# A two-layer streaming encoder step: a tie on the first load of cached keys, the queue of half the key stores, and the instants of the prompt's attention blocks

## Chip, cores and metric

The kernel runs on one core of a Trainium2 chip. The metric is the device time of one launch in microseconds (us), lower is better. The core has a matmul engine (PE, with its weight loads listed as PEld), a vector engine (DVE), a scalar engine (ACT) and GpSimd (POOL); SyncE (SP) only issues DMAs. Each of SP, ACT and POOL issues its DMAs in order; an instruction that waits at the head of an engine's queue holds up all behind it on that engine.

## What is computed

Two layers over 512 prompt rows and 8 x 16 sample rows of width 1024, in float32. Layer 0 is a gated MLP with a spatial mix, layer 1 is attention with a forget bias over 16 heads of 128. The part that matters here is layer 1:

```python
q, k, v, z, logf = fox_project(h, w_in, b_f)          # h: normalised rows; k and v are outputs too
s = q @ k.T * scale + c_q - c_k                        # c: running sum of logf; causal
o = softmax(s) @ v                                     # prompt: 512 keys; sample: 256 cached keys and 16 new ones
x = x + rms_norm((o * silu(z)) @ w_out)
x = x + sigmoid(x @ w_gate) * (p @ w_proj)
```

The outputs are both sets of rows, the new keys and values and log-forget values of both groups, and a state of layer 0.

## The kernel before, in words

Float32 products are split in two parts (`split`, lines 285 to 292: ACT makes the high part, DVE the low part), and a product is three matmuls (`mm3`, 269). The projections of layer 1 use a scheme of seven products on half-sized blocks (`seven_products`, 556): per projection 7 x 4 steps of three matmuls, each step counted as 0.441 planner units. POOL forms the weight sums for it (`left_operands`, 203, line 210), and the weights of layer 1 come by DMAs on POOL's queue (`fetch`, 197), apart from the first four units, which go on SP.

Layer 1 runs in rounds of two heads, p = 0 to 7 (line 1183). A round's steps are the z projection of pair p and the v, k and q projections of pair p + 1; together 4 x 28 x 0.441 = 49.4 units. Beside them, `interleave` (356) traces pieces of attention, each at an instant written by hand in units. Pieces whose instant lies past the last step are traced at the end of the round. The order in which the program is traced is a priority: a scheduler then orders each engine's instructions by its own estimate of when they are ready, and may put a ready one ahead. Where that is not wanted, `queued("sp")` (127) adds an edge: what is traced inside it stays behind `behind["sp"]`, the SP DMA that was traced last (`dma`, 120, sets it), in issue order.

Pieces of a round: two heads of the prompt (`prompt_times`, 1123), each with a setup, four blocks of 128 queries (`scores`, 992), their transposes (`turn`, 7.5 units later) and products with v (`values`, 12.5 later). The first block of the even head is at t0 and a block follows every `step` units; the odd head starts four steps later. `scores` is one matmul group, then on DVE a mask addition (994), an addition with minimum (1004, 1007), the reciprocal (1014) and the scaling (1015), with the exponential on ACT (1010). Then two groups of four sequences of the sample (`sample_times`, 1132). Cached keys come in 32-column pieces, four DMAs per half pair (`load_k`, 1038, on SP, each 128 KB), and DVE turns them (`turn_k`, 1050, line 1054). New keys are stored by `store_k` (919): a DVE transpose (920), then eight DMAs per head, on POOL's queue. The finished head's rows go to DRAM by `store_y` (1136, POOL).

Ahead of the rounds, `tail(0, ...)` ends layer 0: it stores the five residual blocks to `x_sc` on SP (758) as they are done. `project_v0` (885) is the first projection of layer 1; its `weights(2)` (243) takes the first v weights, and with them fetches the next units, the last of them on SP being the k weights of pair 0. Beside it run the forget logits, the sums of h (`right_operands`, 426, line 432: it overwrites the residual's buffers) and the first `load_k(0, 0, 0)`, at 1.0 units, into buffers that the residual blocks used.

Of the kernel before, what the change touches and what calls it, by code (L numbers as in the profile page):

```python
# [57 lines left out]
def hybrid_trunk(tc, x_prompt, x_sample, ck, cv, clf, p_prompt, p_sample, norm_pre, norm_post,  # L58
                 g_win, ln_g, ln_b, w_s, b_s, g_wout, f_win, b_f, f_wout, w_proj, w_gate, consts,
                 y_p, y_s, st_v, fk_p, fv_p, fl_p, fk_s, fv_s, fl_s):  # L60
    nc = tc.nc
# [28 lines left out]
    def r1(o, n, p=P):  # L90
        return R1[:p, o:o + n]
# [11 lines left out]
    def bank(lst=(0, 1, 2, 3, 4, 5, 6, 7)):  # L103
        return PB[ring(("bank", lst), lst)]
# [15 lines left out]
    def dma(out, in_, queue=None):  # L120
        if queue is not None:
            queue.dma_start(out=out, in_=in_)  # L122
        else:
            behind["sp"] = nc.sync.dma_start(out=out, in_=in_)

    @contextmanager
    def queued(*engines):

        with ExitStack() as stack:
            for e in engines:  # L130
                stack.enter_context(tc.issue_after(behind[e].ins))
            yield
# [110 lines left out]
    def weights(n):  # L243

        i0 = state["used"]
        state["used"] += n
        prefetch(i0 + 2 * NW, i0)
        res = []
        for i in range(i0, i0 + n):
            u, j = items[i]  # L250
            k, o, m = units[u][1], place[i][0] * 1024, len(place[i]) * 512
            if u in joined:
                res.append(W[:, o:o + 2 * m].rearrange("p (k n) -> p k n", k=k))
                continue
            if j in (1, 2):
                views = [W[:, o + z:o + z + m].rearrange("p (a k n) -> p k a n", a=2, k=k) for z in (0, m)]
            else:
                views = [W[:, o + z:o + z + m].rearrange("p (k n) -> p k n", k=k) for z in (0, m)]
            res.append(tuple(views))
        return res  # L260
# [69 lines left out]
    def h_at(k, a, b):  # L330
        return h_hi[:, k, a:b], h_lo[:, k, a:b]
# [24 lines left out]
    def interleave(steps, pieces):  # L356


        now, todo = 0.0, sorted(pieces, key=lambda x: x[0])
        for took in steps:  # L360
            now += took
            while todo and todo[0][0] <= now:
                todo.pop(0)[1]()
        for _, piece in todo:
            piece()
# [492 lines left out]
    def v_of(p):  # L858
        return r1(o_v + (p % 2) * 1280, 1280).rearrange("p (t n) -> p t n", t=NT)

    def both(o, i):
        return r1(o + i * TOK, TOK)
# [19 lines left out]
    def store_v(p, t):  # L882
        dma(fv_rows(p, t), v_of(p)[:, t].rearrange("p (h d) -> p h d", h=2))

    def project_v0():
        v = v_of(0)
        ws = weights(2)
        for t in range(NT):
            b = bank(PRJ)
            for k in range(8):  # L890
                w = ws[k // 4][:, k % 4]
                hi, lo = h_at(k, t * P, (t + 1) * P)
                nc.tensor.matmul(b, hi, w, start=k == 0, stop=False)
                nc.tensor.matmul(b[:, :256], lo, w[:, :256], start=False, stop=k == 7)
                if k % 2:
                    yield 0.69
            nc.scalar.activation(out=v[:, t], in_=b[:, 256:], func=AF.Copy)
            nc.vector.tensor_tensor(out=v[:, t], in0=v[:, t], in1=b[:, :256], op=ALU.add)
            store_v(0, t)
# [17 lines left out]
        yield from seven_products(lambda i, j: both(o_vk, i)[:, HALF[j]], lambda i, j, c: None)  # L917

    def store_k(h, tr):
        nc.vector.transpose(out=tr, in_=both(o_k, h % 2))  # L920
        trv = tr.rearrange("p (c d) -> p c d", d=32)
        for qd in range(4):
            dma(fk_p[0, 0, :, h, qd * 32:(qd + 1) * 32].rearrange("(c j) d -> j c d", j=32), trv[qd * 32:(qd + 1) * 32, :16], nc.gpsimd)
            dma(fk_s[0, :, :, h, qd * 32:(qd + 1) * 32].rearrange("(c b) q d -> (b q) c d", c=4), trv[qd * 32:(qd + 1) * 32, 16:], nc.gpsimd)

    def project_k0():
        ws = weights(2)
        n = TOK - SA
        for h in range(2):
            a, b = yield from channel_steps(ws, h, PRJ)  # L930
            kt = both(o_k, h)
            nc.scalar.activation(out=kt[:, :SA], in_=a[:, :SA], func=AF.Copy)
            nc.scalar.activation(out=kt[:, SA:], in_=b[:, n:], func=AF.Copy)
            behind["dve"] = nc.vector.tensor_tensor(out=kt[:, SA:], in0=kt[:, SA:], in1=b[:, :n], op=ALU.add)
            store_k(h, both(o_vk, h))
# [32 lines left out]
    def w0_of(h):  # L968
        return tri if h % 2 else SF[:, 2048:2560] if h < 14 else r1(o_raw, 512)

    def load_w0(h, queue=None):
        dma(w0_of(h), c_sc[h].partition_broadcast(P), queue)
# [65 lines left out]
    def load_k(p, bg, hh):  # L1038
        for qd in range(4):
            d = slice(qd * 32, (qd + 1) * 32)  # L1040
            dma(kraw[d].rearrange("p b (c d) -> p (b c) d", d=32),
                ck[0, 4 * bg:4 * bg + 4, :, 2 * p + hh, d].rearrange("b (c j) d -> j (b c) d", j=32))

    def load_v(p, bg):
        for z in range(2):
            b = 4 * bg + 2 * z
            dma(vv[:, 2 * z:2 * z + 2].rearrange("p b t n -> p (b t) n"),
                cv[0, b:b + 2, :, 2 * p:2 * p + 2, :].rearrange("b (t k) h d -> k (b t) (h d)", k=P))

    def turn_k(p, bg, hh):  # L1050

        with queued("dve"):
            for bl in range(4):
                nc.vector.transpose(out=kt[:, hh, bl, :PAST], in_=kraw[:, bl])  # L1054

    def new_k(p, bg):
        for hh in range(2):
            nc.gpsimd.tensor_copy(out=kt[:, hh, :, PAST:], in_=kn_of(2 * p + hh)[:, 64 * bg:64 * bg + 64].rearrange("p (b k) -> p b k", b=4))
# [64 lines left out]
    def prompt_times(h, t0, step):  # L1123

        setup, scores, turn, values = prompt_pieces(h)
        res = [(t0 - step + 0.1, setup)]
        for i in range(4):
            for after, f in ((0, scores), (7.5, turn), (12.5, values)):
                res.append((t0 + step * i + after, lambda f=f, i=i: f(i)))
        return res  # L1130

    def sample_times(p, bg, t0):
        scores, turn, values, gate = sample_pieces(p, bg)
        return [(t0, scores), (t0 + 7.5, turn), (t0 + 12.5, values), (t0 + 17.5, gate)]

    def store_y(h):
        dma(y_sc[h], y_of(h), nc.gpsimd)
# [12 lines left out]

    def attention_pieces(p, step, s1):

        s0, t0 = 5, 3.2
        pieces = sample_times(p, 0, s0) + sample_times(p, 1, s1)
        ka, kb = 5, 17.6
        pieces += [(s0 + ka, lambda: turn_k(p, 1, 0)), (s0 + ka + 0.1, lambda: load_k(p, 1, 1)), (s0 + kb, lambda: turn_k(p, 1, 1)),
                   (s0 + kb + 0.1, lambda: new_k(p, 1)), (s0 + 13.5, lambda: load_v(p, 1))]
        for hh in range(2):
            pieces += prompt_times(2 * p + hh, t0 + 4 * step * hh, step)
        if p < 7:  # L1160
            pieces += [(s1 + 18, lambda: store_y(2 * p)), (s0 + kb + 0.2, lambda: load_k(p + 1, 0, 0)), (s1 + 13.5, lambda: load_v(p + 1, 0))]
        if p == 6:
            pieces += [(48, lambda: load_w0(14)), (48, lambda: load_w0(15))]
        return pieces

    def next_keys(p, t, t_new):

        return [(t, lambda: turn_k(p, 0, 0)), (t + 0.1, lambda: load_k(p, 0, 1)), (t + 12, lambda: turn_k(p, 0, 1)),
                (t + 12.1, lambda: load_k(p, 1, 0)), (t_new, lambda: new_k(p, 0))]
# [3 lines left out]
    def sums_of_h():  # L1173
        sums.append(right_operands((o_P, o_v + 1280, o_V, o_qp, o_z)))

    interleave(project_v0(), [(0.0, forget_logits), (2.0, log_forget), (2.1, sums_of_h), (9.0, forget_sums),
                              (9.1, lambda: load_w0(0, nc.gpsimd)), (1.0, lambda: load_k(0, 0, 0))])
    interleave(project_k0(), [(11.0, lambda: turn_k(0, 0, 0)), (11.1, lambda: load_k(0, 0, 1)), (0.0, lambda: load_w0(1, nc.gpsimd)), (0.1, lambda: load_mask(0, nc.gpsimd)), (6.0, lambda: load_v(0, 0))])
    split(*quarter(0, 1), sums[0])
    nc.gpsimd.memset(r1(o_qp, 512), 0.0)  # L1180
    interleave(project_q(0), [(8.0, lambda: turn_k(0, 0, 1)),
                              (8.1, lambda: load_k(0, 1, 0)), (12.2, lambda: new_k(0, 0))])
    for p in range(7):
        pieces = attention_pieces(p, 4.7, 26.0) + next_keys(p + 1, 34.0, 46.2)
        pieces += [(26.0, lambda p=p: turn_v(p + 1, 0)), (27.0, lambda p=p: turn_v(p + 1, 1))]
        interleave(project(project_z(p), project_v(p + 1), project_k(p + 1), project_q(p + 1)), pieces)
        store_y(2 * p + 1)
# [4 lines left out]
    pieces = attention_pieces(7, 5.2, 24.7)  # L1192
# [39 lines left out]
```

## Time and profile before

| | us |
|---|---|
| median of 3 runs | 1310.72 (1309.7 to 1311.1) |
| profiled execution, its own time | 1311.3 |
| its span, first to last instruction | 1309.5 |
| PE busy | 1282.0 (98%) |
| DVE busy | 964.2 (74%) |
| ACT busy | 587.7 (45%) |
| POOL busy | 426.7 (33%) |

In lists of groups, a row gives line, engine, operation, out<-in, shapes and count, then busy us, mean ns of one, and the idle time just before them with what ended it. In the timeline a row gives start and duration in us, then the instruction, a count when several follow each other, and in brackets the idle time before it and what ended it. In stretches a row gives the bounds, the length, each engine's busy time with its count, the clock granted to PE as a share of full speed, the busy share of the 16 DMA engines, and GB/s. SPq is SP's queue. Buffers: `R` is the large work buffer, `W` the split weights, `RAW` the weights as they arrive, `pb` the banks of PSUM.

### The profile page before, as it was taken

Reading aid. Unit: us, or ns where it says so; the run is one execution under the profiler, and the core shown is the slowest. Engines: PE = TensorE matmul, PEld = TensorE weight load, DVE = VectorE, ACT = ScalarE, POOL = GpSimd, SP = SyncE. Lnnn points to the kernel's source line nnn. Section 1 sums busy time; section 2 is a strip of 40 time slices with the busy share of each in tenths; the row PEclk is TensorE's granted clock in tenths of the full one; section 3 lists DMA queues with packets and bytes.
Section 4 is the critical chain, followed back from the end, with each engine's and each line's share of the span. In section 5 each row is a group of like instructions: output and inputs, shape, how many; then the busy total and the mean of one; then the engine's idle time right before and its main releaser. Section 6 shows DMA issues by size and latency. Waiting matters only on the chain. (4 is left out here: it accounts for less than half of the span.)

```text
span 1309.5 us, 21108 instructions
## 1 busy us (share of the span) xinstructions
PE 1282.0 (98%) x7873; PEld 1144.3 (87%) x7873; DVE 964.2 (74%) x1808; ACT 587.7 (45%) x1062; POOL 426.7 (33%) x455
## 2 busy tenths in 40 slices
PE   9999999999999999898999999999999999999998
PEld 6888999999988888787898989898988989888887
DVE  7744999999844364696979798988879797744643
ACT  5334555444535343354444354544444454535431
POOL 1012454543000000345554646465545552000100
PEclk9999999999999999998999999999999999999999
DMA  6432334232324213546787667676787667742111
GB/s 228 132 108 67 119 114 127 79 110 75 128 83 160 81 49 103 141 99 139 155 170 154 171 157 174 137 187 126 167 151 167 145 167 209 262 141 81 65 57 57
DMA packets 236353, 171.53 MB, mean 131 GB/s; under 512 B 147801, under 2 KB 198537, under 8 KB 236250
## 3 DMA queue, kind: packets, MB, share of 16 engines
q1 hardware_dynamic: 218162, 122.54, 33.1%
q0 software_dynamic: 14176, 42.14, 15.4%
q10 hardware_dynamic: 3912, 5.50, 1.3%
q8 instruction: 62, 1.02, 0.3%
q14 instruction: 41, 0.34, 0.1%
HBM read 148.55 MB, written 21.59 MB: 130 GB/s over the span
## 5 line engine op out<-in xcount | busy, mean ns | idle before, releaser
L271 PE MATMUL pb<-A,W 128*128 128x320 f32 (+1 forms) x752 | 241.0, 321 | 10.3 <-DVE R L578 4.6
L273 PE MATMUL pb<-A,W 128*128 128x320 f32 (+1 forms) x752 | 235.3, 313 | 0.6 <-DVE W L292 0.6
L272 PE MATMUL pb<-A,W 128*128 128x320 f32 (+1 forms) x752 | 235.7, 313 | 0.0
L289 DVE TENSOR_TENSOR W<-RAW,W 128x1024 fp32r<-128x1024 f32 (+1 forms) x126 | 146.7, 1165 | 85.6 <-ACT W L288 83.4
L271 PE MATMUL pb<-W,A 128*128 128x512 f32 x520 | 205.1, 395 | 0.7 <-ACT A L288 0.7
L272 PE MATMUL pb<-W,A 128*128 128x512 f32 x520 | 204.1, 393 | 0.0
L273 PE MATMUL pb<-W,A 128*128 128x512 f32 x520 | 202.8, 393 | 0.0
L288 ACT ACTIVATE W<-RAW 128x1024 fp32r<-128x1024 f32 (+1 forms) x126 | 120.0, 952 | 107.3 <-PE pb L273 47.0
L271 PEld LDWEIGHTS pb<-A,W 128*128 128x128 f32 x752 | 142.7, 190 | 14.2 <-DVE R L578 5.4
L272 PEld LDWEIGHTS pb<-A,W 128*128 128x128 f32 x752 | 142.8, 190 | 1.3 <-issue 1.2
L273 PEld LDWEIGHTS pb<-A,W 128*128 128x128 f32 x752 | 142.3, 189 | 0.8 <-DVE W L292 0.8
L301 POOL TENSOR_TENSOR SML<-SML 128x1 f32<-128x1 f32 x25 | 18.5, 742 | 372.7 <-DVE SML L299 368.0
L271 PE MATMUL pb<-tbf,W 128*128 128x320 f32 x360 | 117.0, 325 | 0.7 <-ACT W L288 0.3
L273 PEld LDWEIGHTS pb<-W,A 128*128 128x128 f32 x520 | 98.0, 189 | 21.0 <-issue 0.8
L271 PEld LDWEIGHTS pb<-W,A 128*128 128x128 f32 x520 | 98.1, 189 | 20.4 <-ACT A L288 1.1
L272 PEld LDWEIGHTS pb<-W,A 128*128 128x128 f32 x520 | 98.2, 189 | 19.4
L273 PE MATMUL pb<-tbf,W 128*128 128x320 f32 x360 | 112.4, 312 | 1.4 <-DVE W L289 1.2
L272 PE MATMUL pb<-tbf,W 128*128 128x320 f32 x360 | 113.0, 314 | 0.0
L562 DVE TENSOR_TENSOR R<-R,pb 128x320 f32<-128x320 f32 x184 | 85.7, 476 | 23.1 <-PE pb L273 22.0
L210 POOL TENSOR_TENSOR sff<-RAW 128x512 f32<-128x512 f32 x46 | 62.1, 1350 | 88.4 <-DVE W L289 41.1
L122 POOL DMA_DIRECT2D out<-R x128 | 78.2, 618 | 17.2 <-DMA RAW<-in_fox_w_in 10.2
L1010 ACT ACTIVATE R<-R,SML 128x128 f32<-128x128 f32 (+1 forms) x64 | 35.8, 560 | 94.8 <-DVE SML L1007 94.4
(271 smaller groups left out, 2887.9 us busy)
## 6 DMA issues: line engine op xcount, KB each, us to landing
RAW<-in_fox_w_in POOLq DMA_DIRECT2D x46, 512.0 KB, 6.4
RAW<-in_gmlp_w_in SPq DMA_DIRECT2D x40, 512.0 KB
R<-in_cache_fox_k SPq DMA_DIRECT2D x128, 128.0 KB
R<-in_cache_fox_v SPq DMA_DIRECT2D x32, 512.0 KB
RAW<-in_gmlp_w_out SPq DMA_DIRECT2D x16, 512.0 KB
RAW<-in_ple_w_gate SPq DMA_DIRECT2D x16, 512.0 KB
RAW<-in_fox_w_out SPq DMA_DIRECT2D x16, 512.0 KB
R<-in_fox_w_in POOLq DMA_DIRECT2D x14, 512.0 KB, 7.8
```

The source lines that it names most:

```text
L122: queue.dma_start(out=out, in_=in_)
L210: nc.gpsimd.tensor_tensor(out=o, in0=a, in1=b, op=op)
L271: nc.tensor.matmul(out, lh, rh, start=start, stop=False)
L272: nc.tensor.matmul(out, lh, rl, start=False, stop=False)
L273: nc.tensor.matmul(out, ll, rh, start=False, stop=stop)
L288: nc.scalar.activation(out=hi, in_=src, func=AF.Copy)
L289: nc.vector.tensor_tensor(out=lo, in0=src, in1=f(hi), op=ALU.subtract)
L301: nc.gpsimd.tensor_tensor(out=q, in0=t, in1=mhalf, op=ALU.pow)
L562: behind["dve"] = nc.vector.tensor_tensor(out=into(i, j), in0=a, in1=b, op=ALU.add)
L1010: nc.scalar.activation(out=pr[:, :n], in_=pr[:, :n], func=AF.Exp, scale=-1.0, bias=m, accum_out=sm)
```

## The change

Three edits. The first `load_k` of layer 1 is traced inside `queued("sp")`. `store_k` gives its eight DMAs no queue, which means SP, for the even heads from 2 on; heads 0 and 1 and the odd ones stay on POOL. The prompt's first block of a round moves from 3.2 to 4 units in all eight rounds, and the step from 4.7 to 4.8 in rounds 0 to 6 (round 7 keeps 5.2).

```diff
     def store_k(h, tr):
+        queue = nc.gpsimd if h < 2 or h % 2 else None
         nc.vector.transpose(out=tr, in_=both(o_k, h % 2))
         trv = tr.rearrange("p (c d) -> p c d", d=32)
         for qd in range(4):
-            dma(fk_p[...], trv[qd * 32:(qd + 1) * 32, :16], nc.gpsimd)
-            dma(fk_s[...], trv[qd * 32:(qd + 1) * 32, 16:], nc.gpsimd)
+            dma(fk_p[...], trv[qd * 32:(qd + 1) * 32, :16], queue)
+            dma(fk_s[...], trv[qd * 32:(qd + 1) * 32, 16:], queue)
...
     def attention_pieces(p, step, s1):
 
-        s0, t0 = 5, 3.2
+        s0, t0 = 5, 4
...
+    def first_k():
+        with queued("sp"):
+            load_k(0, 0, 0)
+
     interleave(project_v0(), [(0.0, forget_logits), (2.0, log_forget), (2.1, sums_of_h), (9.0, forget_sums),
-                              (9.1, lambda: load_w0(0, nc.gpsimd)), (1.0, lambda: load_k(0, 0, 0))])
+                              (9.1, lambda: load_w0(0, nc.gpsimd)), (1.0, first_k)])
...
     for p in range(7):
-        pieces = attention_pieces(p, 4.7, 26.0) + next_keys(p + 1, 34.0, 46.2)
+        pieces = attention_pieces(p, 4.8, 26.0) + next_keys(p + 1, 34.0, 46.2)
```

More of the change, by code (lines that the diff above doesn't have):

```diff
@@ L922, in store_k @@
         for qd in range(4):
-            dma(fk_p[0, 0, :, h, qd * 32:(qd + 1) * 32].rearrange("(c j) d -> j c d", j=32), trv[qd * 32:(qd + 1) * 32, :16], nc.gpsimd)
-            dma(fk_s[0, :, :, h, qd * 32:(qd + 1) * 32].rearrange("(c b) q d -> (b q) c d", c=4), trv[qd * 32:(qd + 1) * 32, 16:], nc.gpsimd)
+            dma(fk_p[0, 0, :, h, qd * 32:(qd + 1) * 32].rearrange("(c j) d -> j c d", j=32), trv[qd * 32:(qd + 1) * 32, :16], queue)
+            dma(fk_s[0, :, :, h, qd * 32:(qd + 1) * 32].rearrange("(c b) q d -> (b q) c d", c=4), trv[qd * 32:(qd + 1) * 32, 16:], queue)
     def project_k0():
```

## The prediction

> **What bounds the kernel now.** I read the page first, then busy time by stretches, then the waits of the matmul engine (PE).
>
> ```profile
> span 1309.5 us, 21108 instructions
> PE 1282.0 (98%) x7873; PEld 1144.3 (87%) x7873; DVE 964.2 (74%) x1808; ACT 587.7 (45%) x1062; POOL 426.7 (33%) x455
> ```
>
> PE is busy for 98% of the span, so the idle time that any reordering can win back is 1309.5 - 1282.0 = 27.5 us, plus the time that PE ran at a lower clock. The profiled execution took 1311.3 us, 1.8 above its span; the median of the three runs shown is 1310.72, so 0.6 below this execution. The attention loop has eight rounds of two heads, p = 0 to 7. The busy time of rounds 0 to 6, cut where each round's first matmul of the z projection starts:
>
> ```profile
> core 0: us, PE busy (x) PEld busy (x) DVE busy (x) ACT busy (x) POOL busy (x), PEclk, DMA share, GB/s
> 589.05:667.00 77.95, 72.21 (x506) 66.07 (x506) 61.52 (x141) 35.12 (x67) 44.31 (x51) 0.96 0.74 155
> 667.00:738.36 71.36, 69.96 (x508) 63.66 (x507) 61.20 (x139) 32.16 (x65) 42.64 (x49) 1.00 0.77 162
> 738.36:808.66 70.30, 68.27 (x508) 63.58 (x507) 60.97 (x137) 32.41 (x64) 39.33 (x46) 1.00 0.63 155
> 808.66:878.57 69.91, 68.80 (x508) 63.73 (x507) 57.83 (x141) 33.12 (x66) 37.86 (x45) 1.00 0.75 169
> 878.57:950.30 71.73, 69.95 (x508) 63.67 (x507) 62.30 (x139) 32.16 (x65) 41.18 (x48) 1.00 0.70 150
> 950.30:1022.27 71.97, 68.79 (x509) 63.52 (x507) 60.94 (x139) 32.67 (x65) 39.70 (x47) 1.00 0.77 158
> 1022.27:1092.17 69.90, 68.78 (x509) 63.73 (x507) 57.72 (x138) 33.33 (x66) 35.84 (x42) 1.00 0.67 164
> ```
>
> Rounds 1 to 6 lie between 69.90 and 71.97, and round 0 needs 8.05 more than the best. Everything after the start of the loop is therefore worth little per round; the dear spots are ahead of round 0 and in it. PE's two longest waits, from the timeline (start, duration, then the idle time before it and what ended it), and the stretches of 10 us around them:
>
> ```profile
> 551.69 0.44 PE L271 MATMUL pb<-A,W 128*128 128x384 f32 x1 [3.64 <-DVE R L898]
> ```
> ```profile
> 607.88 0.63 PE L271 MATMUL pb<-A,W 128*128 128x320 f32 x1 [3.28 <-DVE R L578]
> ```
> ```profile
> 550.00:560.00 10.00, 8.31 (x44) 7.83 (x45) 9.97 (x12) 0.53 (x1) 0.00 (x0) 0.83 0.15 52
> 600.00:610.00 10.00, 6.72 (x40) 6.46 (x39) 4.28 (x18) 3.71 (x8) 4.96 (x5) 0.84 0.92 199
> 610.00:620.00 10.00, 9.64 (x54) 9.07 (x53) 10.00 (x24) 6.96 (x16) 3.38 (x3) 0.82 0.53 96
> ```
>
> Each time PE waits for the vector engine (DVE). The granted clock (the column after POOL) falls behind both long stalls: 0.17 x 10 = 1.7 us of clock behind the first, 0.16 x 10 + 0.18 x 10 = 3.4 behind the second. Together the two spots cost 3.64 + 1.7 + 3.28 + 3.4 = 12.0 us.
>
> **Part 1, the tie of the first K load: 0 us.** The queue of SyncE (SP) and DVE's wait at this place:
>
> ```profile
> 501.67 8.14 SPq L124 DMA_DIRECT2D RAW<-in_fox_w_in  x4
> ...
> 535.38 5.42 SPq L124 DMA_DIRECT2D R<-in_cache_fox_k  x4
> 540.90 3.08 SPq L124 DMA_DIRECT2D x_sc<-R  x1
> ```
> ```profile
> 549.53 1.78 DVE L432 TENSOR_TENSOR R<-A 128x1280 f32<-128x1280 f32 x1 [7.16 <-issue]
> ```
>
> The four parts of the K load go out ahead of the last residual store (`x_sc`), which is issued 5.5 us later and whose buffer one of the additions of line 432 overwrites. DVE stands still for 7.16 us until 549.53 (the view names no releaser; I read it as that store's landing), and PE's stall of 3.64 follows. A tie behind that store would go at this. But `queued("sp")` ties to `behind["sp"]`, the SP DMA traced last. When `first_k` runs, one step of `project_v0` has been traced, whose `weights(2)` has fetched the units of the first K projection on SP, after `tail` had traced all `x_sc` stores. So the tie is to the last of the four `in_fox_w_in` fetches (501.67 and the 8.14 us after it), and the K load at 535.38 stands behind that already. A tie that the order meets changes no order: SP still issues four K parts, then the store, and no queue is passed. Bounds: 0, and -12.0 if the tie reached the store and both spots vanished. I take 0. What would be late next, had the first stall gone, is the second, which has another cause:
>
> ```profile
> 605.05 0.63 ACT L288 ACTIVATE W<-RAW 128x512 fp32r<-128x512 f32 x1 [8.71 <-DMA RAW<-in_fox_w_in]
> ```
>
> This waits for a weight fetch on POOL's queue, in a stretch where the DMA engines are 0.92 busy; heads 0 and 1 keep their stores on POOL, so nothing here moves.
>
> **Part 2, K stores of heads 2, 4 ... 14 from POOL to SP: -1.0 us.** Eight DMAs per head:
>
> ```profile
> L122 POOL DMA_DIRECT2D out<-R x128 | 78.2, 618 | 17.2 <-DMA RAW<-in_fox_w_in 10.2
> ```
> ```profile
> 933.63 5.00 POOL L122 DMA_DIRECT2D out<-R  x8
> ...
> 947.72 0.76 POOL L122 DMA_DIRECT2D RAW<-in_fox_w_in  x1
> ...
> 951.06 0.57 POOL L122 DMA_DIRECT2D y_sc<-R  x1 [0.38 <-DVE R L1030]
> ```
> ```profile
> 949.72 15.54 DMA R<-in_cache_fox_k
> ```
> ```profile
> L124 SPq DMA_DIRECT2D R<-in_cache_fox_k x98: 312/560/6493, 665.6 to 1091.4; - x98
> ...
>   DVE R L1054: 2.6, 3
> ```
>
> Removed from POOL: 7 x 8 x 0.618 = 34.6 us, 4.9 per round, none of it on PE's path, since POOL is busy for 33%. Added to SP: 56 issues at 0.56 (the median of its K loads), 31 us, also off the path. Queued behind them on SP are the loads of V and K, which are due at 39.5 and 46.1 planner units where the stores come at 35.3, four and eleven units later (a unit is 70 us / 49.4 = 1.42 us), against 8 x 0.56 = 4.5 us of issue; the stores wait only for DVE's transposes of line 920. The gain can come from order: the fetch at 947.72 stands behind sixteen stores, and the K load issued just after it took 15.54 us to land. Five us earlier it would largely be through before the K load starts. DVE waited for K loads 2.6 us in 3 places in rounds 1 to 6: the gain is at most that, plus what the better landing saves downstream. On the other side, the stores now share SP's queue with K loads. If each of the seven heads' stores held the next K load back by those 4.5 us, that would be 31 us of landing; the turns that need it come 12 units (17 us) later, so most is covered, and I bound the loss by the same 2.6. I take -1.0, nearer to the gain, since the fetch and K load of 947 to 965 are in the trace and a wait behind a store is not.
>
> The rule that speaks against this part is in the Trainium skill, DMA: Bandwidth & Descriptors, "Issuing engines are not separate DMA queues": whichever engine starts them, DMAs run on the same 16 DMA engines, and another issuer saves only issue time. By it the sum would be 1.0 higher; no run here separates the two yet.
>
> **Part 3, blocks of the prompt at 4.0 and every 4.8 units: -2.4, and -0.3 in round 0.** The middle of round 3, and four of DVE's groups in that round (count, busy us, mean ns):
>
> ```profile
> 822.66:846.66 24.00, 22.89 (x165) 21.27 (x165) 23.96 (x51) 13.35 (x25) 13.52 (x11) 1.00 0.65 146
> ```
> ```profile
> L1015 DVE TENSOR_SCALAR R<-R,SML 128x128 f32<-128x128 f32 (+3 forms) x8 | 3.9, 485 | 0.1
> L1004 DVE CUSTOM_DVE_ANT_0 R<-pb,sff 128x128 f32<-128x128 f32 (+2 forms) x3 | 1.3, 419 | 1.5 <-PE pb L273 1.5
> L994 DVE TENSOR_TENSOR CST<-CST 128x128 f32<-128x128 f32 x2 | 1.1, 569 | 0.0
> L1014 DVE RECIPROCAL SML<-SML 128x1 f32<-128x1 f32 x8 | 1.2, 152 | 1.4 <-ACT R L1010 1.4
> ```
>
> PE's idle time in this stretch, 24.00 - 22.89 = 1.11 us, is all that the round has (69.91 - 68.80), and DVE is full in it: 23.96 of 24. In the other 45.91 us DVE works 57.83 - 23.96 = 33.87 and has room. Work that is pushed from the full stretch into the last one shortens DVE's backlog. The instants of the blocks in it go from 7.9, 12.6, 17.3, 22.0, 26.7 to 8.8, 13.6, 18.4, 23.2, 28.0 units, 1.1 later on average, 1.56 us. A block's DVE work is the mask addition (0.569), the addition with minimum (0.419, twice except in a head's first block), the reciprocal (0.152) and the scaling (0.485): 8 x 1.625 + 6 x 0.419 = 15.5 us per round, 0.22 us per us. The backlog falls by 1.56 x 0.22 = 0.34 us per round, 2.4 in seven. Bounds: no more than the idle time of rounds 1 to 6 (425.17 - 414.55 busy = 10.6), and as much the other way. In round 0 DVE does a block's work right ahead of the sum that PE waits for at 607.88:
>
> ```profile
> 606.33 0.28 DVE L994 TENSOR_TENSOR R<-sff,CST 128x128 f32<-128x128 f32 x1
> 606.53 0.28 DVE L1004 CUSTOM_DVE_ANT_0 R<-pb,sff 128x128 f32<-128x128 f32 x1
> ```
>
> If the later block falls behind the sum, that saves at most 0.56; I take half.
>
> The last `values` goes from 48.6 to 50.1 units, past the 28 x 4 x 0.441 = 49.4 of the steps, so it is traced at the end of the round. The fourth block also loads a head's mask row on ACT's queue, 1.1 to 1.5 units later now, for a block 35 units on; that is covered. The four matmuls of `values` are only moved; the DVE product behind them and `store_y` of the odd head come about 1.5 units later, 2.1 us. The first z sum that overwrites the stored buffer comes after four products, 7.06 units or 10 us into the round.
>
> ```profile
> y_sc<-R POOLq DMA_DIRECT2D x14, 320.0 KB, 4.5
> ```
>
> In round 5 the store goes out 0.76 us into the round; with 2.1 more and the median landing of 4.5 it is through at 7.4. That hides it by 2.6 us; a landing twice as long would cost DVE 1.9 us in a round, in a stretch where it has room. In round 7 (steps of 5.2) the last `values` goes from 52.1 to 52.9, 7 units ahead of the interleave's end at 59.95; nothing there waits.
>
> Sum: 0 - 1.0 - 2.4 - 0.3 = -3.7, so 1311.3 - 3.7 = 1307.6 for an execution like the profiled one and 1307.0 as a median.
>
> **The rivals.**
> (a) The tie does reach the residual store. For it: DVE's 7.16 us end about where the late store would land. Against: what was traced last on SP. It would give at least the first stall with its clock, 5.3, so 1307.0 - 5.3 = 1301.7, and up to 1295.0. Chance 0.07.
> (b) Round 0's stall shrinks by 0.3 to 0.6 and the clock stays up behind it: -3.4, 1303.6. Against: at 3.28 it already cost 3.4. Chance 0.06. The Trainium skill, TensorE: Matmul & The Clock Gate, part 1, has the clock halve after an idle window of about 3.4 us; the trace has it fall behind a stall of 3.28, so the measurement decides.
> (c) Nothing measurable: POOL's time was free, the backlog is rebuilt in another order, and the two dear spots stay. 1308.1 to 1313.3. Chance 0.22.
> (d) Slower: the first block of the odd head goes from 22.0 to 23.2 units and is now behind the last turn of cached K at 22.6, so that it stands on DVE behind a wait for that K load. The point that decides is a landing of over (22.6 - 10.1) x 1.42 = 17.7 us after the load's due time, and 15.54 has been seen. The price is that each of rounds 1 to 6 takes the pattern of the worst: 6 x 71.97 - 425.17 = +6.7, 1317.4, or half of it, 1314. Against: three waits for K in six rounds. Chance 0.23.
>
> **How the numbers follow.** My forecast has 0.42. About 0.2% (2.6 us) is what a measurement can tell from no change. Faster: 0.42 + 0.07 + 0.06 = 0.55; same 0.22; slower 0.23. The forecast's own range is 1303 to 1308.1; the range given, 1301 to 1315, adds (b), (c) and the nearer half of (a) and (d).
>
> **What would show it.** Right: SP still issues four K parts ahead of the last `x_sc` store near 535, PE still stalls about 3.6 us near 551 and about 3 near 607, clock rows under 0.85 at both; POOL has 72 stores of K and SP 56 more; rounds 1 to 6 near 70.4. Wrong: the store ahead of the K load and no stall at 551 (then (a)); rounds over 72 with DVE waiting for K loads ahead of line 1004 (then (d)); a round 0 under 74 without any change of SP's order.

## The result and the profile after

The changed kernel takes 1298.88 us (median of 6 runs, 1297.73 to 1300.96) against 1310.63 for the kernel before (6 runs beside them): a ratio of 0.9913, 95% interval [0.9901, 0.9926]. That is 11.7 us less, where 3.7 had been forecast, and outside the range. The profiled execution's page begins with the span and the busy time of the engines:

```profile
span 1297.4 us, 21121 instructions
PE 1276.6 (98%) x7873; PEld 1144.2 (88%) x7873; DVE 975.8 (75%) x1808; ACT 588.8 (45%) x1062; POOL 398.8 (31%) x399
```

PE's busy time fell by 5.4 us, though it does the same 7873 matmuls; DVE's rose by 11.6. The rounds, cut at the same matmul as before, are the first seven rows, and the eighth is everything behind them:

```profile
589.14:665.97 76.83, 70.58 (x507) 64.85 (x506) 60.41 (x143) 35.23 (x67) 39.86 (x43) 0.98 0.76 157
665.97:734.82 68.85, 68.23 (x510) 63.71 (x508) 62.13 (x139) 32.84 (x66) 40.35 (x42) 1.00 0.83 174
734.82:802.99 68.17, 68.17 (x510) 63.80 (x508) 62.47 (x139) 32.61 (x66) 34.67 (x39) 1.00 0.69 164
802.99:871.15 68.16, 68.16 (x509) 63.78 (x508) 62.68 (x138) 32.60 (x66) 34.08 (x39) 1.00 0.73 162
871.15:939.76 68.61, 68.37 (x510) 63.73 (x508) 61.93 (x141) 32.61 (x66) 32.93 (x36) 1.00 0.77 152
939.76:1011.87 72.11, 70.06 (x509) 64.67 (x508) 63.47 (x139) 32.73 (x66) 40.31 (x42) 0.98 0.81 171
1011.87:1080.04 68.17, 68.17 (x510) 63.79 (x508) 59.44 (x135) 32.92 (x66) 31.09 (x34) 1.00 0.64 156
1080.04:1297.40 217.36, 213.01 (x1101) 177.99 (x1099) 116.80 (x220) 90.12 (x159) 5.11 (x8) 1.00 0.36 121
```

The loop starts where it did (589.14 against 589.05) and what follows the seven rounds is as long (217.36 against 1309.5 - 1092.17 = 217.33). The whole gain lies in the rounds: 1080.04 - 589.14 = 490.90 against 503.12. In three of them PE has no idle time left, and they are shorter than PE's *busy* time was before (68.17 against 68.27 to 69.96). Only round 5 stayed at 72.

What the tie should have touched is where it was. SP's queue, then PE's two long stalls, then the stretches of 10 us around them:

```profile
535.23 5.44 SPq L124 DMA_DIRECT2D R<-in_cache_fox_k  x4
540.77 3.45 SPq L124 DMA_DIRECT2D x_sc<-R  x1
```
```profile
551.79 0.69 PE L271 MATMUL pb<-A,W 128*128 128x384 f32 x1 [3.96 <-DVE R L898]
...
607.73 0.41 PE L271 MATMUL pb<-A,W 128*128 128x320 f32 x1 [3.19 <-DVE R L578]
```
```profile
550.00:560.00 10.00, 8.21 (x44) 7.71 (x45) 9.96 (x12) 0.43 (x1) 0.06 (x1) 0.83 0.15 52
600.00:610.00 10.00, 6.73 (x42) 6.20 (x42) 4.44 (x18) 3.88 (x9) 4.89 (x5) 0.97 0.92 198
610.00:620.00 10.00, 9.11 (x52) 8.19 (x51) 10.00 (x24) 6.80 (x14) 3.53 (x4) 0.86 0.55 98
```

Four K parts still go ahead of the last residual store, and both stalls are there. Behind the second the granted clock lost 0.3 + 1.4 = 1.7 us where it had lost 3.4. Round 0 is 1.1 us shorter (76.83 against 77.95).

Where the rounds differ is seen in the stretch from 3.5 to 14 us into round 3, first before, then after (the fifth column is DVE):

```profile
812.16:822.66 10.50, 10.50 (x83) 9.66 (x82) 5.96 (x21) 1.86 (x6) 5.80 (x7) 1.00 0.68 159
```
```profile
806.49:816.99 10.50, 10.50 (x82) 9.66 (x81) 9.76 (x25) 3.95 (x8) 4.25 (x6) 1.00 0.47 115
```

DVE had a hole here, 5.96 us of work in 10.5, right ahead of the 24 us in which it is full (23.96 of 24). Now the hole is filled, and ACT does twice as much in it. The work that moved in is the split of the next weights (ACT line 288, DVE 289), which needs POOL's sums of line 210. POOL's timeline around the same place, before and after:

```profile
813.00 0.76 POOL L122 DMA_DIRECT2D R<-in_fox_w_in  x1 [2.33 <-issue]
815.02 0.24 POOL L1058 COPY R<-R 128x64 f32<-128x64 f32 x1 [1.26 <-PE pb L1078]
...
815.68 1.29 POOL L210 TENSOR_TENSOR sff<-RAW 128x512 f32<-128x512 f32 x1
817.05 1.30 POOL L210 TENSOR_TENSOR sff<-sff,RAW 128x512 f32<-128x512 f32 x1
818.43 1.30 POOL L210 TENSOR_TENSOR sff<-RAW,sff 128x512 f32<-128x512 f32 x1
```
```profile
801.87 1.27 POOL L210 TENSOR_TENSOR sff<-RAW 128x512 f32<-128x512 f32 x1 [0.95 <-DVE W L289]
...
804.85 1.41 POOL L210 TENSOR_TENSOR sff<-sff,RAW 128x512 f32<-128x512 f32 x1
...
807.00 1.30 POOL L210 TENSOR_TENSOR sff<-RAW,sff 128x512 f32<-128x512 f32 x1
```

Round 3 starts at 808.66 before and at 802.99 after. The second to fourth sums of this set came 7.0 to 9.8 us into the round and now come from 1.1 us ahead of it to 4.0 us into it.

### The profile page after: what moved, and what is told of

It is laid out like the page before. It is cut to its first block, busy times and chain, and to the rows that moved or that the text cites. A ratio compares the mean times of both kernels' runs of the same rounds, so it can differ in the third digit from the quotient of the medians.

```text
span 1297.4 us, 21121 instructions
## 1 busy us (share of the span) xinstructions
PE 1276.6 (98%) x7873; PEld 1144.2 (88%) x7873; DVE 975.8 (75%) x1808; ACT 588.8 (45%) x1062; POOL 398.8 (31%) x399
## 4 chain that ended last, share of the span: by engine, by line
PE 44%; DVE 4%; DMA 2%; issue 1%; POOL 1%; ACT 0%; DVEq 0%; SPq 0%; ACTq 0%
PE pb L271 12%; PE pb L272 12%; PE pb L273 12%; PE pb L1029 2%; PE pb L1022 1%; PE pb L1106 1%; DMA RAW<-in_fox_w_in 1%; DVE W L289 1%; PE pb L1079 1%; DVE R L1055 1%; DMA R<-in_fox_w_in 1%; PE pb L906 1%; DVE R L959 0%; POOL sff L210 0%; DMA R<-in_cache_fox_k 0%
## 5 line engine op out<-in xcount | busy, mean ns | idle before, releaser
L289 DVE TENSOR_TENSOR W<-RAW,W 128x1024 fp32r<-128x1024 f32 (+1 forms) x126 | 160.9, 1278 | 80.4 <-ACT W L288 77.7
L289 DVE TENSOR_TENSOR A<-R,A 128x640 fp32r<-128x640 f32 (+1 forms) x42 | 34.4, 854 | 58.2 <-ACT A L288 58.2
L271 PEld LDWEIGHTS pb<-tbf,W 128*128 128x128 f32 x360 | 68.1, 189 | 9.3 <-issue 6.2
```

Source lines behind the costliest of these rows:

```text
L271: nc.tensor.matmul(out, lh, rh, start=start, stop=False)
L289: nc.vector.tensor_tensor(out=lo, in0=src, in1=f(hi), op=ALU.subtract)
```

## The experiments

**The three parts alone.** Each is the kernel before with one part of the diff. The first has the tie:

```diff
+    def first_k():
+        with queued("sp"):
+            load_k(0, 0, 0)
```

> Part 1 alone on the kernel before. Theory (the tie is to a weight fetch that SP issues earlier anyway): ratio 1.000 within 0.1%, PE stalls of about 3.6 us near 551 and 3.2 near 607 stay, SP issues the four K parts ahead of the last x_sc store. Rival (the tie reaches the store): 5 to 12 us faster, and the stall near 551 is gone.

1310.44 us against 1310.46, ratio 1.0001 [0.9992, 1.0011]. The tie does nothing.

The second has the stores:

```diff
+        queue = nc.gpsimd if h < 2 or h % 2 else None
```

> Part 2 alone on the kernel before (even heads' K stores on SP, instants as before). POOL theory: the eight store issues are what held POOL's weight sums (line 210) back; without them the sums stand about 8 us earlier in a round, the splits fill the idle stretch of DVE 4 to 14 us into the round, and most of the 11.7 us comes: 1299 to 1303. Instants theory (part 3 of the prediction carries the gain): at most 1 to 2 us, 1308 to 1310.

1290.88 us (1290.62 to 1291.23), ratio 0.9851 [0.9835, 0.9868]: 19.6 us less, more than the whole change. Rounds 1 to 4 and 6 are alike to 0.01 us and PE never waits in them (one of them):

```profile
801.21:868.65 67.44, 67.44 (x509) 63.60 (x507) 59.95 (x137) 32.42 (x65) 35.07 (x38) 1.00 0.74 163
```

The third has the instants:

```diff
-        s0, t0 = 5, 3.2
+        s0, t0 = 5, 4
...
-        pieces = attention_pieces(p, 4.7, 26.0) + ...
+        pieces = attention_pieces(p, 4.8, 26.0) + ...
```

> Part 3 alone on the kernel before (first block at 4.0, step 4.8; all K stores on POOL). POOL theory: little, 1307 to 1313, the idle stretch of DVE at 4 to 14 us of a round stays. Instants theory: most of the 11.7 us, 1299 to 1303. If neither alone brings it (both near 1310), the two only work together.

1313.59 us, ratio 1.0022 [1.0013, 1.0032]: slower by 3.1. One place alone has 3.64 us (at 703.50): a group of the sample's matmuls waits there for a turn of cached K (line 1054). The row is the kernel's whole group:

```profile
L1078 PE MATMUL pb<-R 128*32 128x272 f32 x256 | 24.0, 407 | 4.6 <-DVE R L1054 3.6 <-DMA R<-in_cache_fox_k 0.6 <-DVE R L1118 0.3
```

So the parts are 0, -19.6 and, on top of the second, 1298.88 - 1290.88 = +8.0.

**A tie that reaches the store.** The changed kernel, and then part 2 alone, with the tie to the residual store itself:

```diff
             dma(x_sc[t], x1[t])
+            behind["store"] = behind["sp"]
...
-        with queued("sp"):
+        with queued("store"):
```

> The changed kernel with the first K load tied behind the last residual store itself (the store's DMA is remembered and used for the tie). Theory: SP issues the store about 5 us earlier, DVE's wait ahead of line 432 falls from 7 to 1 or 2 us, the stall of 3.96 near 551 and its 1.7 us of clock go: 5 us faster than the changed kernel, 1294; if the later stall near 607 goes too, 1287 to 1289. Rival (another wait takes the place: DVE is full from 550 to 590 and the stall near 607 waits for a weight fetch): 1296 to 1299.

> Part 2 alone with the tie behind the residual store itself, instants as before. Theory: the two gains add up, 1290.9 - 2.2 (the 2.2 that this tie won on the changed kernel) = 1288.7; with the first stall and its clock won in full 1286. Rival: the later stalls of round 0 and the round after it grow by what is won, 1290 to 1292.

1296.64 us (1295.42 to 1298.55; ratio to before 0.9896 [0.9882, 0.9911]), and 1288.21 us (0.9828 [0.9812, 0.9845]): 2.2 and 2.7 less than without the tie. In the second kernel SP's queue now has the stores first, PE has no idle time from 550 to 560 and keeps its clock, but the second stall is longer than before:

```profile
530.24 8.45 SPq L124 DMA_DIRECT2D x_sc<-R  x2
538.86 6.72 SPq L124 DMA_DIRECT2D R<-in_cache_fox_k  x3
```
```profile
550.00:560.00 10.00, 10.00 (x64) 8.74 (x63) 9.97 (x8) 4.40 (x6) 4.67 (x3) 1.00 0.14 49
```
```profile
604.50 0.63 PE L271 MATMUL pb<-A,W 128*128 128x320 f32 x1 [3.92 <-DVE R L578]
```

The loop starts 3.5 us earlier (585.18 against 588.64), and round 0 gives 1.1 back.

**Which queue takes the stores, and which heads'.** On part 2 alone: the even heads' stores on ACT's queue; then those of all heads from 2 on on SP; then the odd heads' in place of the even ones':

```diff
+        queue = nc.gpsimd if h < 2 or h % 2 else nc.scalar
...
+        queue = nc.gpsimd if h < 2 else None
...
+        queue = nc.gpsimd if h < 2 or h % 2 == 0 else None
```

> Part 2 alone, but the even heads' K stores go on ACT's queue and not on SP's. POOL theory: it is enough that they leave POOL; ACT has room, so 1289 to 1294. Rival (SP is the point, or ACT pays for eight issues per round that stand ahead of its copies): over 1297.

> Part 2 extended: the K stores of all heads from 2 on, odd ones too, go on SP; instants as before. POOL theory in its simple form: eight more issues off POOL per round win a little more, 1286 to 1290. Rival (the sums already stand early enough, DVE's idle stretch is filled, nothing is left to win; SP's queue now holds sixteen stores ahead of the next K load): 1290 to 1296.

> The instants of before, no tie; now the stores of the odd heads go to SP and those of the even heads stay on POOL. POOL has as many stores as with part 2 alone, in the same order beside the other operations, except that they stand one sum earlier. If it counts how many stores POOL carries (its time, the order that goes with it): 1290 to 1293 us. If the even heads' stores, ahead of the last sum of a set, are the costly ones: 1300 to 1311 us.

1291.76 us (0.9858 [0.9844, 0.9873]), 1295.75 (0.9885 [0.9865, 0.9905]) and 1293.71 (0.9871 [0.9853, 0.9888]). ACT's queue is as good as SP's, so what counts is that the stores leave POOL. Which eight of a round leave matters little (16.4 us won with the odd heads'), and moving the other eight as well gains nothing (its four runs lie between 1291.86 and 1298.33).

**POOL's time.** Is it the time that the stores' issue takes on POOL? On part 2 alone, products of one column stand in for the even heads' stores. The first try had one product that reads the turned K and seven that read a constant:

```diff
+        queue = nc.gpsimd if h < 2 or h % 2 else None
...
+        if queue is None:
...
+            nc.gpsimd.tensor_tensor(out=PAD[:, 7:8], in0=tr[:, :1], in1=one, op=ALU.mult)
+            for z in range(7):
+                nc.gpsimd.tensor_tensor(out=PAD[:, z:z + 1], in0=one, in1=mhalf, op=ALU.pow)
```

> Part 2 alone, but POOL gets eight dummy instructions of one column (about 0.7 us each, about 5 us per round) at each place where the eight stores left it; the stores are on SP. POOL theory: the time on POOL is what counts, so most of the 19.6 us that part 2 alone won is lost again, 1303 to 1311. Rival (the stores' DMAs, or the completion counters that the weight fetches share with them on POOL's queue, were the cost, not POOL's time): stays at 1290 to 1294.

1294.85 us (0.9881 [0.9866, 0.9895]). The scheduler took the 49 that depend on nothing to the program's start, as the group's first and last start show (17.6 and 49.7 us), so only one product per even head was left in the rounds:

```profile
L928 POOL TENSOR_TENSOR PAD<-CST,SML x49: 541/545/1612, 17.6 to 49.7; 128x1 f32<-128x1 f32 x49
```

Then each product was made to read a column of the turned K, eight of them and then twenty:

```diff
+            for z in range(8):
+                nc.gpsimd.tensor_tensor(out=PAD[:, z:z + 1], in0=tr[:, z:z + 1], in1=one, op=ALU.mult)
```

> Part 2 alone, plus eight one-column products on POOL for every even head from 2 on, each reading a column of the turned K that the eight stores read, so that they cannot be taken ahead of it (56 in all; those that stood at their place in the earlier try took 0.67 us each, so 5.4 us per round, where the stores took 4.9). If POOL's time at this place is the price (the weight sums of line 210 come later by as much), 10 us or more of the 19.6 us won comes back: 1300 to 1311 us, with rounds of 69.5 to 71.5. If it is the stores themselves that cost (their landings, and the waits of the POOL queue for the completion of earlier transfers), the time stays at 1291 to 1293 with rounds of 67.45.

> As the try with eight products of one column, with twenty of them for every even head; eight took 2.65 us, so these take 6.6, above the 4.9 of the eight stores. POOL's order is that of part 2 alone. If POOL's time at this place costs by the microsecond: well over the 3.9 us of the eight, 1300 us or more. If what counts is only that the sums are ready before the splits want them, and the order: 1295 to 1298 us, rounds of 67.45 to 68.5.

1294.82 us (0.9883 [0.9869, 0.9897]) and 1300.04 us (0.9919 [0.9903, 0.9934]): 3.9 and 9.2 us given back. The eight took 18.7 us of POOL in all. The twenty took this, and the stores of K took what the second fence has, part 2 alone (before: 78.2):

```profile
L927 POOL TENSOR_TENSOR PAD<-R,CST 128x1 f32<-128x1 f32 x140 | 34.7, 288 | 0.0
```
```profile
L122 POOL DMA_DIRECT2D out<-R x72 | 43.6, 612 | 32.1 <-DMA RAW<-in_fox_w_in 24.7 <-issue 3.7 <-DVE SML L1015 3.0
```

The twenty did not take the 6.6 us per round that I had reckoned but 34.7 / 7 = 5.0, as good as what the 56 stores took, 78.2 - 43.6 = 34.6. Not all of the 9.2 us is the price of POOL's time in the rounds, though. The profiled executions, cut at the matmuls where rounds 0 and 7 start, in us:

| | ahead of the rounds | rounds 0 to 6 | behind them |
|---|---|---|---|
| part 2 alone | 588.64 | 483.25 | 217.31 |
| first try | 591.19 | 482.16 | 218.65 |
| eight products | 589.81 | 484.44 | 218.65 |
| twenty products | 589.23 | 491.00 | 218.87 |

What lies behind the rounds is 1.3 to 1.6 us longer in all three, also in the first try, which loses nothing in the rounds; why is open. Inside the rounds the eight give back 1.2 us and the twenty 7.8. So POOL's time there, with the order that the scheduler makes around it, is worth about 7.8 of the 19.6 us, and it has no fixed price per microsecond. The hole of round 3 does not come back with them: with the twenty products it stays nearly filled, in the same stretch from 3.5 to 14 us into the round:

```profile
807.84:818.34 10.50, 10.50 (x83) 9.67 (x82) 9.16 (x27) 4.12 (x9) 5.98 (x8) 1.00 0.56 147
```

The waits of the remaining stores for earlier transfers are not what part 2 won: they went up, from 17.2 us (the row in the prediction) to 32.1, while the kernel became faster.

**The order alone.** The kernel before, all stores on POOL, with the copies of line 1058 ordered behind the sums:

```diff
-                nc.gpsimd.tensor_tensor(out=o, in0=a, in1=b, op=op)
+                behind["sum"] = nc.gpsimd.tensor_tensor(out=o, in0=a, in1=b, op=op)
...
+        with queued("sum"):
             for hh in range(2):
                 nc.gpsimd.tensor_copy(out=kt[:, hh, :, PAST:], ...)
```

> The kernel before with all its stores on POOL's queue; the only edit is an order: the copies of new keys into the cached K (line 1058) are ordered behind the last weight sum that was written before them, as they mostly are where the even stores are off POOL. If the order of POOL's program is the price (sums of line 210 behind two copies that wait for PE), much of the 19.6 us comes without any store moved: 1291 to 1300 us, rounds of 67.4 to 69. If POOL's time or the stores' landings are, it stays within 3 us of before: 1307 to 1313 us.

1325.68 us, ratio 1.0116 [1.01, 1.0132]: 15.6 us slower, which neither theory had. Most of it is one wait: PE's wait for DVE's line 1007 ahead of the sample's `values` (line 1103) has 12.0 us in six places, where the kernel before has 1.6 in two (line 1102 there). The last sum of the set starts 6.5 us into round 3 in place of 9.8, and the traces say why this didn't help. POOL's sum, ACT and DVE in round 3, which starts at 812.28:

```profile
818.80 1.29 POOL L210 TENSOR_TENSOR sff<-RAW,sff 128x512 f32<-128x512 f32 x1
```
```profile
825.48 0.28 ACT L1023 ACTIVATE R<-pb 128x128 f32<-128x128 f32 x1 [5.25 <-PE pb L1021]
...
827.97 1.04 ACT L288 ACTIVATE W<-sff 128x1024 fp32r<-128x1024 f32 x1
```
```profile
824.87 0.89 DVE L562 TENSOR_TENSOR R<-R,pb 128x320 f32<-128x320 f32 x2 [2.34 <-PE pb L273]
```

The set is ready at 820.09, 7.8 us into the round, but its split starts at 827.97, because in ACT's own order it stands behind an eviction that waits 5.25 us for PE. DVE has only 5.35 us of work in the 10.5 us from 3.5 us into the round. A sum fills the hole only if the split that uses it has been placed ahead of the work that waits for PE, in ACT's and DVE's orders too. With part 2 that is so: ACT's split of the same set there starts 5.7 us into the round,

```profile
806.89 1.04 ACT L288 ACTIVATE W<-sff 128x1024 fp32r<-128x1024 f32 x1
```

while POOL's sums were under way. All these orders come from the scheduler. That it places the splits earlier because POOL is free sooner is my reading; no run shows it by itself.

**What in the instants costs 8.0.** Part 2 with one of the two numbers, then with half the shift of the first:

```diff
+        s0, t0 = 5, 4
...
+        pieces = attention_pieces(p, 4.8, 26.0) + ...
...
+        s0, t0 = 5, 3.6
```

> Part 2 and the first block at 4.0, steps left at 4.7. The two instants together cost 8.0 us on top of part 2 (1298.88 against 1290.88). At 4.0 alone the odd head's first block (22.8 units) is behind the last turn of cached K (22.6) and the last product with v (49.40) falls just past the last step (49.39); at 4.8 alone neither happens (22.4 and 49.3). If these crossings are the price, this run takes most of the 8.0: 1296 to 1300 us. If it is the mere shift of the blocks against the weights' splits, each edit costs by the shift that it makes (0.8 unit here, 0.35 in the mean there): some 5.5 us here, 1296 us, and 2.5 us in the other.

> Part 2 and steps of 4.8, the first block left at 3.2. If the crossings are the price: 1290.5 to 1292 us, as part 2 alone. If the shift is: 1293 to 1294 us.

> Part 2 and the first block at 3.6, half the shift: 22.4 units for the odd head's first block (ahead of the last turn of cached K at 22.6) and 49.0 for the last product with v (ahead of the end at 49.39). The shift to 4.0 cost 9.3 us. If the crossings are the price: 1290.5 to 1292.5 us. If the shift is: about 4.6 us, 1295.5 us.

1300.21 us (0.9925 [0.9911, 0.9939]), 1294.17 (0.9875 [0.9861, 0.9889]) and 1291.72 (0.9856 [0.984, 0.9871]) against 1290.88. The first block at 4.0 costs 9.3 us, at 3.6 only 0.8, which is within the noise, so it is not the shift as such, which would have been half. Steps of 4.8 cost 3.3, more than my crossings allowed, and the two together less than their sum. Most of the 8.0 has a place. A round has two groups of 16 matmuls of 32 columns each, the sample's `values`. PE around the first of them in the changed kernel, and with part 2 alone, in round 3:

```profile
824.24 0.63 PE L1106 MATMUL pb<-R 128*32 128x256 f32 x4
824.79 0.44 PE L1022 MATMUL pb<-CST,R 128*128 128x128 f32 x2
825.16 1.06 PE L1106 MATMUL pb<-R 128*32 128x256 f32 x12
826.15 0.41 PE L271 MATMUL pb<-tbf,W 128*128 128x320 f32 x1
```
```profile
820.23 0.38 PE L1022 MATMUL pb<-CST,R 128*128 128x128 f32 x2
820.37 0.39 PE L272 MATMUL pb<-A,W 128*128 128x320 f32 x1
...
824.02 1.07 PE L1106 MATMUL pb<-R 128*32 128x256 f32 x16
825.02 0.41 PE L273 MATMUL pb<-tbf,W 128*128 128x320 f32 x1
```

With the block at 4.0 a pair of a block's transposes (line 1022) falls inside the group. From its first matmul to the next product it then takes 1.91 us in place of 1.00. With part 2 alone a pair stands among the products, where the next one starts 0.14 us after it. Rounds 2, 3 and 6, in which PE waits in neither kernel, give the whole price of a broken group: 68.16 or 68.17 us against 67.44, so 0.72. One group is broken in each of rounds 1 to 6, which makes 4.3 us; with part 2 alone none is. In rounds 1, 4 and 5 the pair also waits for its block, 2.8 us in all, and the rest of the group with it. Behind the longest of these waits, in round 5, the granted clock falls:

```profile
961.60 0.63 PE L1106 MATMUL pb<-R 128*32 128x256 f32 x4
963.94 0.44 PE L1022 MATMUL pb<-CST,R 128*128 128x128 f32 x2 [1.71 <-DVE R L1016]
```
```profile
960.00:965.00 5.00, 3.29 (x25) 1.99 (x26) 5.00 (x10) 0.60 (x2) 3.69 (x4) 0.94 0.31 44
965.00:970.00 5.00, 5.00 (x27) 3.91 (x22) 3.74 (x10) 3.44 (x7) 1.30 (x1) 0.72 0.80 109
```

That is 0.3 + 1.4 = 1.7 us of clock. The three together, 8.8 us, are about the 8.5 us by which rounds 1 to 6 are longer than with part 2 alone (414.07 against 405.56). The 3.3 us of the steps alone are not settled: no group is broken there.

The kernel before has such breaks too, seven in rounds 0 to 6, where part 2 alone has one. The whole groups' rows, before and with part 2 alone:

```profile
L1105 PE MATMUL pb<-R 128*32 128x256 f32 x256 | 21.4, 387 | 0.0
```
```profile
L1106 PE MATMUL pb<-R 128*32 128x256 f32 x256 | 17.7, 385 | 0.0
```

**Better versions.** Three more, all with the tie to the store and part 2: all stores of K on SP (heads 0 and 1 too), the first block at 3.6, and at 2.4.

```diff
-        queue = nc.gpsimd if h < 2 or h % 2 else None
+        queue = None
...
+        s0, t0 = 5, 3.6
...
+        s0, t0 = 5, 2.4
```

> All stores of new K on SP, heads 0 and 1 too, and the first load of cached K tied behind the residual store itself; the instants of before. Beside the best run so far (part 2 alone with that tie, 1288.21 us) only the stores of heads 0 and the odd ones leave POOL. If the stall near 607 us comes from the weight fetch that POOL issues behind the stores of heads 0 and 1, it goes, with 3 to 7 us: 1281 to 1285 us. If it is another wait, the time stays at 1288, or goes up by what all stores on SP cost before (1295.75 against 1290.88 with heads 2 and up on SP): 1288 to 1293 us.

> The best run so far (part 2 alone and the first load of cached K tied behind the residual store itself, 1288.21 us) with the first block at 3.6, which without the tie gave 1291.72 us beside 1290.88, but seven rounds of 480.6 us where the others had 483.3 and 484.8. If the shorter rounds are real and the tie takes the stall at 551 us away as before: 1284 to 1288 us. If what the rounds win is lost in the last round again: 1288 to 1290 us.

> The same with the first block at 2.4. If the time only falls when the blocks stay ahead of the two crossings, it is 1288 to 1290 us; if each shift of the blocks re-orders the program for better or worse, it can be as far off as the 9.3 us of the other direction: up to 1297 us.

1292.05 us (1287.86 to 1294.88; 0.9859 [0.984, 0.9878]), 1287.55 (0.9826 [0.9812, 0.9839]) and 1287.34 (0.9822 [0.9808, 0.9836]). With all stores on SP, ACT's wait for a weight fetch ahead of the stall near 607 (8.46 us with part 2 and the tie to the store) is gone. But DVE waits 4.71 us there for a mask row (`sff<-c_sc`, line 996), and PE stalls for 2.80 us, at 606.97, behind DVE's line 1009: another late transfer has taken the place of the first. The last two can't be told from 1288.21. All three kernels of 1287 to 1288 beat both kernels of this study, by 22 to 23 us and by 11.

## Why the prediction was wrong

**Part 1 was right.** The tie meets an order that is there already, costs and wins nothing (ratio 1.0001), and both stalls stayed with about their lengths. Rival (a) gave 1301.7 to 1295.0, which holds the measured time, but its mechanism didn't happen. Made to happen, it wins 2.2 to 2.7, not the 5.3 to 12.0 that I gave it: the first stall and its clock go, and what is late next, the second, stays at 3.7 to 3.9 us, as the prediction had said.

**Part 2 is the step that failed**: "none of it on PE's path, since POOL is busy for 33%", so "-1.0". It measured -19.6. I had followed the stores to the fetch and the K load behind them on the DMA queues, and had taken a third of busy time as proof that POOL's time is free. But the sums of line 210 stand in POOL's program among the stores, ACT's and DVE's splits need the sums, and DVE has a hole of 4.5 us ahead of its full stretch into which the splits fit if they are ready. POOL's 34.6 us are worth about 7.8 as time (twenty products, in the rounds). About 3.7 of the 19.6 are the broken groups of `values`, which the kernel before has (21.4 us against 17.7) and which stay whole with the twenty products, so that they are not among the 7.8. What the other 8.1 are I can't say. That the hole stays filled with the twenty products speaks for the order of the splits, which changed with the stores; but no run changed that order by itself in the right direction.

The Trainium skill, DMA: Bandwidth & Descriptors, "Issuing engines are not separate DMA queues", says that another issuer only saves the time to initiate the DMA, usually small beside the DMA itself. By it this part was to win nothing. The runs agree that the other queue matters little: ACT's does as well as SP's. But the time to initiate, 0.618 us per store and 34.6 us in all, was not small here; what it costs depends on what stands behind the issue on that engine.

**The bounds failed with it.** The prediction held that no more than PE's idle time, 10.6 us in rounds 1 to 6, could be won there. With part 2 alone these rounds take 1071.89 - 666.33 = 405.56 us, less than the 414.55 that PE was *busy* in them before. Busy time is no floor: of the 19.6 us that these rounds won, 10.2 were idle time (10.62 against 0.44) and 9.4 had counted as busy (414.55 against 405.12). A broken group counts as busy, which is about 3.7 of it. The ends of matmuls are modelled, too: a product's record lasts 0.31 us while the next starts some 0.15 us after its start (at 825.27 and 825.41 in round 3 of part 2 alone), so a short wait between two products shows as busy. How much of the rest this is was not worked out.

**Part 3 had the wrong sign.** I reckoned with 0.22 us of DVE work per us of shift and a backlog that falls by 0.34 us per round; it cost 3.1 us alone and 8.0 on part 2. Work was not what decided. The instants also decide which piece stands next to which in each engine's order, and at 4.0 two transposes break the sample's group and make it wait for their block. Rival (d) had the sign and a wait for cached K; alone, part 3 does have one such wait, of 3.64 us, but on the sample's matmuls and once.

**Of what was to show it**: the order on SP, the stalls of 3.96 and 3.19 us and the 72 stores on POOL came; the clock stayed below 0.85 at the first stall only (0.83, then 0.97 and 0.86); and the rounds were at 68.2 to 68.9 and one at 72.1, not near 70.4. The stall in round 0 shrank by 0.09 us, not by the 0.3 of the sum. That the clock lost 1.7 us less behind it is no mark of the later block: with part 2 alone it lost 1.7 there as well (0.86 and 0.97 in the same two stretches).

## What to carry to other kernels

A low busy share doesn't make an engine's time free: look at what stands behind an instruction in that engine's order, and whether an engine that is full later has a hole just ahead in which it could have used the result. Here POOL was the wrong place for half of the stores of K; SP, which only issues DMAs, and ACT did equally well. And try the parts of a change alone: here one was worth more than the whole, and another had eaten 8.0 of its 19.6 us.

## What the runs showed of the hardware

Sixteen matmuls of 32 columns, 385 ns each, run in 1.07 us together; a group that a pair of other matmuls breaks costs 0.72 us more. Behind a wait of PE of only 1.71 us the granted clock was 0.72 over 5 us.

The same stores make other packets on another queue. The DMA queues before and after (packets, MB, share of the 16 engines' time):

```profile
q1 hardware_dynamic: 218162, 122.54, 33.1%
q0 software_dynamic: 14176, 42.14, 15.4%
```
```profile
q1 hardware_dynamic: 236978, 124.84, 34.3%
q0 software_dynamic: 12384, 39.84, 15.0%
```

The 2.30 MB of the 56 stores were 1,792 packets on POOL's queue (q0) and are 18,816 on SP's (q1). From the shares and the spans (1309.5 and 1297.4 us), POOL's queue took about 7 us less of the 16 DMA engines' time and SP's about 12 us more. The second is a rough estimate, since with the tie alone, where the packets are those of before, SP's share is 33.4% already. PE's weight loads waited for these stores once in the changed kernel, for 0.3 us.
